# Gated MLPs by fast matrix products: factors of the second token half made form by form between the products, and the down-projection's sums moved to VectorE

## Chip, cores and metric

The kernel runs on one core of a Trainium2 chip. The metric is the device time of one execution in microseconds. The core has TensorE (PE, matmuls into PSUM), VectorE (DVE), ScalarE (ACT), GpSimd (POOL) and the queue of SyncE (SP) that issues its transfers between HBM and SBUF.

## What is computed

A trunk of two layers over 1024 tokens of 1024 channels in float32: a gated linear attention layer, then a differential attention layer on shared keys and values, each followed by the same kind of gated MLP with a causal convolution of width 3 over the tokens. The change touches the two MLPs alone. From the reference:

```python
def conv_ffn(h, w_in, conv_w, conv_b, w_out):
    S = h.shape[1]
    u = h @ w_in                                  # 1024 -> 2 x 2816
    up = jnp.pad(u, ((0, 0), (CONV_WIDTH - 1, 0), (0, 0)))
    c = sum(up[:, j:j + S, :] * conv_w[j] for j in range(CONV_WIDTH)) + conv_b
    a, g = jnp.split(c, 2, axis=-1)
    return (jax.nn.silu(g) * a) @ w_out           # 2816 -> 1024
...
h = h + conv_ffn(rmsnorm(h, ffn_norm_w[l]), ffn_w_in[l], ffn_conv_w[l], ffn_conv_b[l], ffn_w_out[l])
```

## The kernel before

Channels lie on the 128 partitions and tokens on the free axis, in two halves of 512 tokens. A float32 product is made of three matmuls: each operand x is split into a rounded high part (copied by ScalarE) and a low part x - high (made by VectorE), and high x high, low x high and high x low are summed in PSUM. `halves` makes such a pair for a tile of 128 x 512: one ScalarE row, one VectorE row.

Both projections of an MLP use a seven-product scheme for 2 x 2 block matrices (Winograd's form of Strassen's). In the up-projection a block product is formed of sums of weight blocks (the pieces `wp`, made by `pieces` and `pieces_by_form`, their sums on GpSimd) and sums of blocks of the normalised stream (the factors `xp`). The blocks of the stream are channel halves and token halves: b11 and a21 (first token half), b12 and b22 (second). The seven factor forms are called "11", "21", "22", "t1", "t2", "t3", "t4"; each has four tiles. "11" and "21" need the first token half alone and are ready when the MLP starts. The other five need the second half, whose RMS norm is finished by `nm.begin(1)` and `nm.end(1)` during the first two products; `nm.factors1()` then makes all five forms in one go, 8 scalings (`scaled`), 16 subtractions in place and 20 pairs of halves.

A product is 12 matmuls of 128 x 512 (four tiles, three matmuls each). `product(i, n)` takes the next weight piece with `take()`, which also makes the piece four products ahead (`AHEAD = WIN`), and `mid(i, n, o)` adds the result to the tiles `u` of pair i. The first two tile pairs (i = 0, 1) are computed together, in the order of forms 11, 21, 22, t1, t2, t3, t4, each form for both pairs: these are products 0 to 13, and the text counts them so. From product 14 on, pairs i = 2 to 21 follow one by one, with the convolutions (`conv_a`, `conv_g0`, `conv_g1`) of the pair before; beside i = 2 run the convolutions of pairs 0 and 1.

In the down-projection seven products n = 0 to 6 run over 11 steps j each; a step is four units (d) of three matmuls. `factors(n, j)` is called two steps ahead and makes the weight factor `lp` and the activation factor `rp` of a step; E[j] and O[j] are the even and odd tile of W_out (`wo`), and for n = 1, 2, 4 a factor is a sum of them (`ws` or `wo` in place). `gather(n, d)` takes the outputs of product n to the residual tiles `h` (from `ht`): products 0 and 1 are copied to `pt` tiles t1 and t2 by ScalarE, and with product 2 the shared sums p1 (product 0 + 2) and p7 (p1 + product 1) go to the four output blocks h11, h12, h21, h22.

The orders of PE, ACT and the SP queue are those of the program text. DVE and POOL rows are put in order by the framework's scheduler, but run in that order. All work tiles come from one pool of 44 slots, U(...).

## Time and profile before

| | us |
|---|---|
| median of three runs | 2475.18 (2474.60 to 2475.31) |
| the profiled execution | 2473.61 |
| its span, first to last instruction | 2471.9 |
| PE busy | 2341.2 (95%) |
| DVE busy | 1899.2 (77%) |
| ACT busy | 1039.0 (42%) |
| POOL busy | 837.4 (34%) |
| mean granted TensorE clock | 0.978 of 2.4 GHz |

Busy shares are means over stages with different limits; what a stage waits for is read from that stage. The first MLP begins near 455 us and ends near 1130, the second runs from 1763 to the end. A timeline row gives start, duration, engine, line, operation and tiles (out<-in, buffer numbers left out), and in brackets the idle time ahead of it and what ended it. A DVE or ACT row that stands among others of its engine overlaps the next by 0.08 to 0.1 us, so rows are counted from start to start.

### The profile page before, as it was taken

What the parts mean: (1) busy time and instruction counts of PE and PEld (TensorE: products, weight loads), DVE (VectorE), ACT (ScalarE), POOL (GpSimd) and SP (SyncE); (2) the same over time, 40 slices, a digit from 0 to 9 for tenths busy, and PEclk for the clock granted to TensorE, in tenths of its full rate; (3) what the DMA queues carried; (4) which work ended last, traced back from release to release, by engine and by line L of the source; (5) the groups of instructions that cost most, each with busy time, mean ns of one, the idle gap of its engine ahead of it and who ended that gap; (6) DMA issues with size and microseconds to landing.
All of it is one profiled execution on the core that took longest, in us unless ns stands there. A gap on an engine that the chain in (4) does not pass through costs nothing. (4 is left out here: it accounts for less than half of the span.)

```text
span 2471.9 us, 29625 instructions
## 1 busy us (share of the span) xinstructions
PE 2341.2 (95%) x10926; PEld 1888.5 (76%) x10926; DVE 1899.2 (77%) x2509; ACT 1039.0 (42%) x1856; POOL 837.4 (34%) x659
## 2 busy tenths in 40 slices
PE   8999999799999998999999999899789999998998
PEld 6878877577888886788877777787667888886786
DVE  7454454779999998957148888776779999999966
ACT  5433442433444344444124555544334433343453
POOL 3210101145554428400004444522036545436501
PEclk9999999899999999999999999999989999999999
DMA  4011224122333356324243333522113323256422
GB/s 178 1 52 69 70 93 149 42 68 95 111 110 99 111 200 230 117 71 165 81 138 106 107 111 95 182 75 94 67 34 120 119 82 111 92 192 222 144 88 98
DMA packets 101426, 271.22 MB, mean 110 GB/s; under 512 B 10273, under 2 KB 23201, under 8 KB 101281
## 3 DMA queue, kind: packets, MB, share of 16 engines
q1 hardware_dynamic: 101280, 269.34, 32.3%
q8 instruction: 85, 1.39, 0.2%
q14 instruction: 61, 0.49, 0.1%
HBM read 184.89 MB, written 76.02 MB: 106 GB/s over the span
## 5 line engine op out<-in xcount | busy, mean ns | idle before, releaser
L896 PE MATMUL pf<-xp,wp 128*128 128x512 f32 x1232 | 489.2, 397 | 37.4 <-ACT wp L205 33.2
L897 PE MATMUL pf<-xp,wp 128*128 128x512 f32 x1232 | 489.0, 397 | 7.1 <-DVE wp L114 7.1
L898 PE MATMUL pf<-xp,wp 128*128 128x512 f32 x1232 | 488.6, 397 | 0.0
L896 PEld LDWEIGHTS pf<-xp,wp 128*128 128x128 f32 x1232 | 233.1, 189 | 94.0 <-ACT wp L205 34.3
L897 PEld LDWEIGHTS pf<-xp,wp 128*128 128x128 f32 x1232 | 233.1, 189 | 64.3 <-DVE wp L114 9.1
L898 PEld LDWEIGHTS pf<-xp,wp 128*128 128x128 f32 x1232 | 233.0, 189 | 54.8
L1007 PE MATMUL out<-rp,lp 128*128 128x512 f32 (+1 forms) x632 | 251.1, 397 | 19.1 <-DVE rp L114 18.8
L1006 PE MATMUL out<-rp,lp 128*128 128x512 f32 (+1 forms) x632 | 250.1, 396 | 6.3 <-DVE lp L114 6.3
L114 DVE SCALAR_TENSOR_TENSOR c<-u,cv,c 128x1024 f32<-128x1024 f32 x176 | 244.7, 1392 | 7.6 <-ACT c L903 7.6
L1005 PE MATMUL out<-rp,lp 128*128 128x512 f32 (+1 forms) x632 | 249.9, 395 | 0.6 <-ACT rp L205 0.6
L111 DVE TENSOR_TENSOR u<-pf,u 128x512 f32<-128x512 f32 x300 | 200.4, 679 | 28.3 <-PE pf L898 20.1
L114 DVE SCALAR_TENSOR_TENSOR wp<-raw,wp 128x512 fp32r<-128x512 f32 x180 | 203.0, 1139 | 12.9 <-ACT wp L205 12.9
L275 PE MATMUL pf<-xh,wh 128*128 128x512 f32 x458 | 187.5, 409 | 10.7 <-ACT wh L195 9.7
L276 PE MATMUL pf<-xh,wl 128*128 128x512 f32 x458 | 181.9, 397 | 1.2 <-DVE wl L114 1.2
L277 PE MATMUL pf<-xl,wh 128*128 128x512 f32 x458 | 181.4, 396 | 0.0
L1007 PEld LDWEIGHTS out<-rp,lp 128*128 128x128 f32 x632 | 121.3, 192 | 51.6 <-DVE rp L114 24.6
L111 POOL TENSOR_TENSOR rs_y<-rs_m,nhalf 128x4 f32<-128x4 f32 (+2 forms) x26 | 31.9, 1226 | 370.9 <-DVE rs_m L291 301.7
L923 ACT ACTIVATE c<-c 128x1024 f32<-128x1024 f32 x44 | 46.7, 1061 | 255.7 <-DVE c L114 255.7
L114 DVE SCALAR_TENSOR_TENSOR wp<-wt,wp 128x512 fp32r<-128x512 f32 x128 | 153.6, 1204 | 0.0
L1006 PEld LDWEIGHTS out<-rp,lp 128*128 128x128 f32 x632 | 120.8, 191 | 36.8 <-DVE lp L114 9.8
L111 POOL TENSOR_TENSOR wt<-raw,wt 128x512 f32<-128x512 f32 x40 | 57.0, 1425 | 254.5 <-DVE wp L114 254.5
L1005 PEld LDWEIGHTS out<-rp,lp 128*128 128x128 f32 x632 | 121.3, 192 | 27.6 <-ACT rp L205 1.1
(252 smaller groups left out, 5170.5 us busy)
## 6 DMA issues: line engine op xcount, KB each, us to landing
raw<-in_w_in SPq DMA_DIRECT2D x88, 512.0 KB, 4.2
tr<-td SPq DMA_DIRECT2D x70, 512.0 KB, 4.1
td<-c SPq DMA_DIRECT2D x44, 512.0 KB, 2.8
wo<-in_w_out SPq DMA_DIRECT2D x44, 512.0 KB, 8.5
raw<-in_w_gla SPq DMA_DIRECT2D x24, 512.0 KB, 5.9
h<-hs SPq DMA_DIRECT2D x24, 512.0 KB, 6.5
td<-mt SPq DMA_DIRECT2D x22, 512.0 KB, 3.8
hs<-h SPq DMA_DIRECT2D x32, 256.0 KB, 2.0
```

The lines of the kernel that those rows point to most:

```text
L111: eng.tensor_tensor(out=o, in0=a, in1=b, op=op)
L114: eng.scalar_tensor_tensor(out=o, in0=a, scalar=s, in1=b, op0=op0, op1=op1)
L275: PE.matmul(o, wh[:, k], xh[:, H(hf)], start=(k == 0), stop=False)
L276: PE.matmul(o, wl[:, k], xh[:, H(hf)], start=False, stop=False)
L277: PE.matmul(o, wh[:, k], xl[:, H(hf)], start=False, stop=(k == ND - 1))
L896: PE.matmul(o, wh, xh, start=(k == 0), stop=False)
L897: PE.matmul(o, wl, xh, start=False, stop=False)
L898: PE.matmul(o, wh, xl, start=False, stop=(k == ND // 2 - 1))
L923: ACT.activation(gt, gt, AF.Silu)
L1005: PE.matmul(o, wh, xh, start=(j == 0 or cut and j == NJ - LASTF), stop=False)
L1006: PE.matmul(o, wl, xh, start=False, stop=False)
L1007: PE.matmul(o, wh, xl, start=False, stop=(j == NJ - 1 or cut and j == NJ - LASTF - 1))
```

## The change

`factors1` becomes `factor1(q)`, which makes one form. `WHEN` says behind which product each is made: "22" behind product 1, t1 behind 2, t2 behind 4, t3 behind 6, t4 behind 8; the scalings of the second token half are made with "22" (four) and t1 (four). The `mid` of a product now stands behind the factor that is made there.

In the down-projection the sums of `factors` for n = 1, 2 and 4 go from GpSimd to VectorE. Product 2's outputs are copied by ScalarE to tiles t3, as those of products 0 and 1 are, and its twelve sums with the shared terms leave `gather`: `shared(d, part)` makes them on VectorE, one part behind each of the steps j = 1 to 8 of product 3.

```diff
@@ -35,6 +35,7 @@
 EX = 2
 SK = 1
 PF = (4, 4)
+WHEN = {1: "22", 2: "t1", 4: "t2", 6: "t3", 8: "t4"}
 CV = (2, 3, 4, 5)
 VGP = 4
 OGP = 4
@@ -392,27 +393,22 @@
 
             self.f["11" if d < ND // 2 else "21"].append(halves(self.scaled(d, 0), "xp"))
 
-        def factors1(self):
-
-            f, n = self.f, ND // 2
-            a1, a2 = ([self.x[q * n + d][:, H(0)] for d in range(n)] for q in range(2))
-            b2 = [self.scaled(n + d, 1) for d in range(n)]
+        def factor1(self, q):
+
+            n = ND // 2
+            a1, a2 = ([self.x[p * n + d][:, H(0)] for d in range(n)] for p in range(2))
+            b1, b2 = ([self.x[p * n + d][:, H(1)] for d in range(n)] for p in range(2))
+            if q in ("22", "t1"):
+                for d in range(n):
+                    self.scaled(d if q == "t1" else n + d, 1)
+            to, x, y = {"22": (b2, None, None), "t1": (a1, b1, a1), "t2": (a1, b2, a1), "t3": (b1, b2, b1),
+                        "t4": (a2, a2, a1)}[q]
             for d in range(n):
-                f["22"].append(halves(b2[d], "xp"))
-            b1 = [self.scaled(d, 1) for d in range(n)]
-            for d in range(n):
-                tt(DVE, a1[d], b1[d], a1[d], ALU.subtract)
-                f["t1"].append(halves(a1[d], "xp"))
-            for d in range(n):
-                tt(DVE, a1[d], b2[d], a1[d], ALU.subtract)
-                f["t2"].append(halves(a1[d], "xp"))
-            for d in range(n):
-                tt(DVE, b1[d], b2[d], b1[d], ALU.subtract)
-                f["t3"].append(halves(b1[d], "xp"))
-            for d in range(n):
-                tt(DVE, a2[d], a2[d], a1[d], ALU.subtract)
-                f["t4"].append(halves(a2[d], "xp"))
-            self.x.clear()
+                if x is not None:
+                    tt(DVE, to[d], x[d], y[d], ALU.subtract)
+                self.f[q].append(halves(to[d], "xp"))
+            if q == "t4":
+                self.x.clear()
 
     class Late:
 
@@ -954,7 +950,7 @@
         CG = (2, 4, 6, 7, 10)
         SRC = (0, 1, 5, 4, 3, 6, 2)
         E, O, lp, rp, rraw, acc, ht = {}, {}, {}, {}, {}, {}, []
-        t1, t2 = {}, {}
+        t1, t2, t3 = {}, {}, {}
 
         def load_w(f):
             t = (O if f % 2 else E)[f // 2] = U("wo")
@@ -974,16 +970,16 @@
                 x = a[0]
             elif n == 1:
                 x = U("ws")[:, H(0)]
-                tt(POOL, x, a[0], a[1], ALU.subtract)
+                tt(DVE, x, a[0], a[1], ALU.subtract)
             elif n == 2:
                 x = a[0]
-                tt(POOL, a[1], a[1], b[1], ALU.add)
+                tt(DVE, a[1], a[1], b[1], ALU.add)
                 tt(DVE, x, a[1], x, ALU.subtract)
             elif n == 3:
                 x = a[1]
             elif n == 4:
                 x = a[0]
-                tt(POOL, x, b[0], x, ALU.subtract)
+                tt(DVE, x, b[0], x, ALU.subtract)
                 del E[j]
             elif n == 5:
                 x = b[1]
@@ -1006,27 +1002,32 @@
             PE.matmul(o, wl, xh, start=False, stop=False)
             PE.matmul(o, wh, xl, start=False, stop=(j == NJ - 1 or cut and j == NJ - LASTF - 1))
 
+        def shared(d, part):
+
+            h11, h12, h21, h22 = (ht[k][:, H(q)] for k in (d, d + 4) for q in range(2))
+            p1, p7, p6 = (t[d // 2][:, H(d % 2)] for t in (t1, t2, t3))
+            if part == 0:
+                tt(DVE, p6, p1, p6, ALU.add)
+                tt(DVE, p7, p6, p7, ALU.add)
+                tt(DVE, h12, h12, p6, ALU.add)
+                return
+            tt(DVE, h22, h22, p7, ALU.add)
+            tt(DVE, h21, h21, p7, ALU.add)
+            tt(DVE, h11, h11, p1, ALU.add)
+            if d % 2 == 1:
+                del t1[d // 2], t2[d // 2], t3[d // 2]
+
         def gather(n, d, sl=H(0)):
 
             o = acc.pop((n, d))
-            if n < 2:
-                t = (t1, t2)[n]
+            if n < 3:
+                t = (t1, t2, t3)[n]
                 if d % 2 == 0:
                     t[d // 2] = U("pt")
                 ACT.activation(t[d // 2][:, H(d % 2)], o, AF.Copy)
                 return
             h11, h12, h21, h22 = (ht[k][:, H(q)] for k in (d, d + 4) for q in range(2))
-            if n == 2:
-                p1, p7 = t1[d // 2][:, H(d % 2)], t2[d // 2][:, H(d % 2)]
-                tt(POOL, h11, h11, p1, ALU.add)
-                tt(DVE, p1, o, p1, ALU.add)
-                tt(DVE, p7, p1, p7, ALU.add)
-                tt(POOL, h12, h12, p1, ALU.add)
-                tt(POOL, h21, h21, p7, ALU.add)
-                tt(DVE, h22, h22, p7, ALU.add)
-                if d % 2 == 1:
-                    del t1[d // 2], t2[d // 2]
-            elif n == 3:
+            if n == 3:
                 tt(DVE, h12, o, h12, ALU.add)
                 tt(DVE, h22, o, h22, ALU.add)
             elif n == 4:
@@ -1039,12 +1040,14 @@
 
         AHEAD = WIN
         for k, (n, i) in enumerate((n, i) for n in (0, 2, 6, 4, 1, 3, 5) for i in range(2)):
-            mid(i, n, product(i, n))
+            o = product(i, n)
             if k == 0:
                 nm.begin(1)
             if k == 1:
                 nm.end(1)
-                nm.factors1()
+            if k in WHEN:
+                nm.factor1(WHEN[k])
+            mid(i, n, o)
         for i in range(2, NF):
             for p, n in enumerate(range(7)):
                 if i == NF - 1:
@@ -1110,6 +1113,8 @@
             for d in range(4):
                 unit(n, j, d)
             del lp[n, j], rp[n, j]
+            if n == 3 and 1 <= j < 9:
+                shared((j - 1) % 4, (j - 1) // 4)
             if j == NJ - 1:
                 for d in range(4):
                     gather(n, d)
```

The order of ScalarE at the start of an MLP's up-projection, before: the last five of the 20 factor copies (`xp`), then the weight pieces (`wp`) of products 6 to 9 with the copies of products 4 and 5 (`u`) between them.

```order
L205 ACTIVATE xp_3589<-h_2961 128x512
L205 ACTIVATE xp_3593<-h_2987 128x512
L205 ACTIVATE xp_3597<-h_3038 128x512
L205 ACTIVATE xp_3601<-h_3125 128x512
L205 ACTIVATE wp_3604<-wt_3084 128x512
L205 ACTIVATE wp_3625<-wt_3088 128x512
L205 ACTIVATE wp_3642<-wt_3084 128x512
L854 ACTIVATE u_3457<-pf_3645 128x512
L205 ACTIVATE wp_3659<-wt_3088 128x512
```

The same place after the change, from the first copy for form "22" on.

```order
L206 ACTIVATE xp_3523<-h_2961 128x512
L206 ACTIVATE xp_3526<-h_2987 128x512
L206 ACTIVATE xp_3529<-h_3038 128x512
L206 ACTIVATE xp_3532<-h_3125 128x512
L846 ACTIVATE u_3490<-pf_3496 128x512
L206 ACTIVATE wp_3536<-wt_3084 128x512
L206 ACTIVATE xp_3561<-h_2950 128x512
L206 ACTIVATE xp_3565<-h_2974 128x512
L206 ACTIVATE xp_3569<-h_3000 128x512
L206 ACTIVATE xp_3573<-h_3082 128x512
L206 ACTIVATE wp_3577<-wt_3088 128x512
L206 ACTIVATE wp_3594<-wt_3084 128x512
```

Product 6's piece (the first `wp<-wt`) stands behind four factor copies, and the pieces of products 7 and 8 behind four more.

GpSimd at the start of product 1 of the first MLP's down-projection, before: the sum `ws` of each step and the first sum of product 2, in turn.

```order
L111 TENSOR_TENSOR ws_7006<-wo_6671 128x512
L111 TENSOR_TENSOR wo_6671<-wo_6671,wo_6982 128x512
L111 TENSOR_TENSOR ws_7032<-wo_6690 128x512
L111 TENSOR_TENSOR wo_6690<-wo_6690,wo_7002 128x512
L111 TENSOR_TENSOR ws_7062<-wo_6713 128x512
L111 TENSOR_TENSOR wo_6713<-wo_6713,wo_7030 128x512
```

VectorE at the same place, before, from the last row of product 0 (`rp<-c`) on.

```order
L114 SCALAR_TENSOR_TENSOR rp_6987<-c_6709,rp_6987 128x512
L114 SCALAR_TENSOR_TENSOR lp_7008<-ws_7006,lp_7008 128x512
L114 SCALAR_TENSOR_TENSOR rp_7011<-tr_6962,rp_7011 128x512
L111 TENSOR_TENSOR wo_6671<-wo_6671 128x512
L111 TENSOR_TENSOR wo_6690<-wo_6690 128x512
L114 SCALAR_TENSOR_TENSOR lp_7034<-ws_7032,lp_7034 128x512
L114 SCALAR_TENSOR_TENSOR rp_7037<-tr_6962,rp_7037 128x512
L111 TENSOR_TENSOR wo_6713<-wo_6713 128x512
```

VectorE there after the change; the rows of GpSimd are gone.

```order
L115 SCALAR_TENSOR_TENSOR rp_6987<-c_6709,rp_6987 128x512
L112 TENSOR_TENSOR ws_7006<-wo_6671 128x512
L112 TENSOR_TENSOR wo_6671<-wo_6671,wo_6982 128x512
L115 SCALAR_TENSOR_TENSOR lp_7008<-ws_7006,lp_7008 128x512
L115 SCALAR_TENSOR_TENSOR rp_7011<-tr_6962,rp_7011 128x512
L112 TENSOR_TENSOR wo_6671<-wo_6671 128x512
L112 TENSOR_TENSOR ws_7032<-wo_6690 128x512
L112 TENSOR_TENSOR wo_6690<-wo_6690,wo_7002 128x512
L115 SCALAR_TENSOR_TENSOR lp_7034<-ws_7032,lp_7034 128x512
L115 SCALAR_TENSOR_TENSOR rp_7037<-tr_6962,rp_7037 128x512
L112 TENSOR_TENSOR wo_6690<-wo_6690 128x512
```

A step of product 1 on VectorE is now five rows: `ws`, the add with the odd tile, `lp`, `rp`, and product 2's subtraction.

VectorE at the start of product 3, before: the shared output sums of product 2 (tiles `pt` and `h`) between `lp` and `rp` of step 3.

```order
L114 SCALAR_TENSOR_TENSOR lp_7612<-wo_6735,lp_7612 128x512
L111 TENSOR_TENSOR pt_7052<-out_7334,pt_7052 128x512
L111 TENSOR_TENSOR pt_7052<-out_7338,pt_7052 128x512
L111 TENSOR_TENSOR pt_7316<-pt_7052,pt_7316 128x512 x2
L111 TENSOR_TENSOR h_7350<-h_7350,pt_7316 128x512
L111 TENSOR_TENSOR h_7372<-h_7372,pt_7316 128x512
L111 TENSOR_TENSOR pt_7055<-out_7342,pt_7055 128x512
L111 TENSOR_TENSOR pt_7055<-out_7346,pt_7055 128x512
L111 TENSOR_TENSOR pt_7319<-pt_7055,pt_7319 128x512 x2
L111 TENSOR_TENSOR h_7396<-h_7396,pt_7319 128x512
L111 TENSOR_TENSOR h_7418<-h_7418,pt_7319 128x512
L114 SCALAR_TENSOR_TENSOR rp_7615<-tr_7526,rp_7615 128x512
```

After the change, from `lp` of step 1 of product 3 on.

```order
L115 SCALAR_TENSOR_TENSOR lp_7546<-wo_6690,lp_7546 128x512
L115 SCALAR_TENSOR_TENSOR rp_7549<-tr_7484,rp_7549 128x512
L112 TENSOR_TENSOR pt_7564<-pt_7052,pt_7564 128x512 x2
L112 TENSOR_TENSOR pt_7316<-pt_7564,pt_7316 128x512
L112 TENSOR_TENSOR h_7248<-h_7248,pt_7564 128x512
L112 TENSOR_TENSOR pt_7316<-pt_7564,pt_7316 128x512
L115 SCALAR_TENSOR_TENSOR lp_7572<-wo_6713,lp_7572 128x512
L115 SCALAR_TENSOR_TENSOR rp_7575<-tr_7526,rp_7575 128x512
L115 SCALAR_TENSOR_TENSOR lp_7594<-wo_6735,lp_7594 128x512
L115 SCALAR_TENSOR_TENSOR rp_7597<-tr_7526,rp_7597 128x512
L115 SCALAR_TENSOR_TENSOR lp_7617<-wo_6752,lp_7617 128x512
L115 SCALAR_TENSOR_TENSOR rp_7620<-tr_7570,rp_7620 128x512
```

The block is split: five rows stand ahead of step 2's `lp` and `rp`, the others come between later steps.

## Rows read from the trace of the kernel before

**Rows 1.** Waits of PE over the span: us in total, times, longest.

```profile
PE pf L896 <- ACT wp L205: 33.2, 2, 16.6
PE out L1007 <- DVE rp L114: 18.8, 10, 5.6
...
PE pf L897 <- DVE wp L114: 7.1, 4, 2.0
PE out L1006 <- DVE lp L114: 6.3, 8, 1.3
```

**Rows 2.** Timeline of PE, start of the second MLP's up-projection.

```profile
1800.36 0.79 PE L896 MATMUL pf<-xp,wp 128*128 128x512 f32 x1 [16.62 <-ACT wp L205]
1802.75 0.80 PE L897 MATMUL pf<-xp,wp 128*128 128x512 f32 x1 [1.60 <-DVE wp L114]
1803.34 0.63 PE L898 MATMUL pf<-xp,wp 128*128 128x512 f32 x1
...
1808.03 0.39 PE L897 MATMUL pf<-xp,wp 128*128 128x512 f32 x1
1808.26 0.40 PE L898 MATMUL pf<-xp,wp 128*128 128x512 f32 x1
...
1874.30 0.51 PE L897 MATMUL pf<-xp,wp 128*128 128x512 f32 x1 [1.88 <-DVE wp L114]
```

**Rows 3.** Timeline of ACT, same stretch: product 6's piece, product 14's copy.

```profile
1799.70 1.65 ACT L205 ACTIVATE wp<-wt 128x512 fp32r<-128x512 f32 x3
...
1830.31 0.60 ACT L868 ACTIVATE u<-pf 128x512 f32<-128x512 f32 x1 [13.34 <-PE pf L898]
```

**Rows 4.** Timeline of DVE, same stretch: first and last factor rows, then pieces.

```profile
1772.64 2.73 DVE L114 SCALAR_TENSOR_TENSOR h<-h,gains_sb,rb 128x512 f32<-128x512 f32 x4 [1.12 <-PE rb L308]
1775.28 2.49 DVE L114 SCALAR_TENSOR_TENSOR xp<-h,xp 128x512 fp32r<-128x512 f32 x4
...
1798.98 1.28 DVE L111 TENSOR_TENSOR u<-pf,u 128x512 f32<-128x512 f32 x2
...
1800.95 4.64 DVE L114 SCALAR_TENSOR_TENSOR wp<-wt,wp 128x512 fp32r<-128x512 f32 x4
```

**Rows 5.** Windows, down-projections: length, busy by engine, PE clock, DMA share, GB/s.

```profile
950.00:1000.00 50.00, 42.85 (x168) 32.50 (x169) 45.63 (x41) 19.69 (x37) 39.09 (x24) 0.97 0.53 187
1000.00:1050.00 50.00, 44.40 (x180) 35.39 (x179) 47.07 (x56) 23.52 (x41) 19.74 (x13) 0.93 0.37 107
...
2250.00:2300.00 50.00, 43.59 (x165) 32.60 (x164) 45.59 (x39) 21.07 (x39) 40.65 (x26) 0.93 0.63 229
2300.00:2350.00 50.00, 44.43 (x181) 35.45 (x180) 47.64 (x52) 19.99 (x36) 25.29 (x16) 0.93 0.35 104
```

**Rows 6.** Timelines of DVE, ACT and POOL, second MLP, end of product 0, product 1.

```profile
2240.72 1.78 DVE L114 SCALAR_TENSOR_TENSOR rp<-c,rp 128x512 fp32r<-128x512 f32 x1
...
2250.17 1.22 ACT L1016 ACTIVATE pt<-out 128x512 f32<-128x512 f32 x2 [0.15 <-PE out L1007]
...
2250.19 1.63 POOL L111 TENSOR_TENSOR wo<-wo,wo 128x512 f32<-128x512 f32 x1
...
2254.00 1.78 DVE L111 TENSOR_TENSOR wo<-wo 128x512 f32<-128x512 f32 x1
2255.70 1.78 DVE L114 SCALAR_TENSOR_TENSOR lp<-ws,lp 128x512 fp32r<-128x512 f32 x1
```

**Rows 7.** Timelines of DVE and PE, second MLP, product 3.

```profile
2322.68 1.28 DVE L111 TENSOR_TENSOR pt<-out,pt 128x512 f32<-128x512 f32 x2
...
2337.86 0.68 DVE L114 SCALAR_TENSOR_TENSOR rp<-tr,rp 128x512 fp32r<-128x512 f32 x1
...
2338.59 0.80 PE L1007 MATMUL out<-rp,lp 128*128 128x512 f32 x1 [5.57 <-DVE rp L114]
```

**Rows 8.** Timeline of POOL, start of the second MLP's up-projection.

```profile
1799.20 1.28 POOL L111 TENSOR_TENSOR wt<-raw 128x512 f32<-128x512 f32 x1 [29.08 <-DVE h L111]
1800.56 1.59 POOL L111 TENSOR_TENSOR wt<-wt,raw 128x512 f32<-128x512 f32 x1
```

## The prediction

> **What bounds the kernel now.** I read the waits of TensorE first, over the whole span: who made it stand still, and for how long [rows 1]. Four of these lines belong to the two MLPs: 33.2 us in two waits for a piece of up-projection weights, 7.1 us for the low half of such a piece, and 18.8 + 6.3 us for the factors rp and lp of the down-projection. That is 65 of the 2471.9 us. The rest of the MLPs runs TensorE without a gap, so these 65 us, and the half clock that follows them, are all that an edit of this kind can win.
>
> Then I went to the two places. At the up-projection's start the second MLP's timeline [rows 2] shows TensorE, with six products done, idle for 16.62 us up to 1800.36, a second wait of 1.60, and then 0.427 us from matmul to matmul until 1808.03 ((1808.03 - 1803.34) / 11): half clock, 1.2 GHz, against 0.23 at the full 2.4 just after. So 16.6 + 1.6 idle and 12 x (0.427 - 0.23) = 2.4 lost to the clock, 20.5 us; the first MLP has the same two waits (the counts of 2 and 4 in [rows 1]). What was late is product 6's weight piece, which ScalarE copied at 1799.70, right after the last of its 20 copies for factors [rows 3]. Those copies waited for VectorE, which from 1772.64 to 1798.98 made nothing but factors [rows 4].
>
> In the down-projection I read windows of 50 us [rows 5]. In each MLP the two windows around products 1 and 3 hold PE busy of 42.6 to 44.4 of 50: 12.8 us idle in the first MLP, 12.0 in the second, and a mean clock of 0.93 to 0.97, which is another (0.03 + 0.07) x 50 = 5.0 and 7.0 us at most (some of that low clock falls in the idle time itself; from the half-rate bursts that follow the waits I count 4 and 6). So 17 to 18 us for each MLP, say 17.5. Why: in product 1 each VectorE row takes 1.70 us from start to start [rows 6], although a low half of the same size takes 0.60 when GpSimd rests (four in 2.49, the last of them 0.68 long [rows 4]); GpSimd is in a sum all that time. Three such rows for a step are 5.1 us, and a step of TensorE is 12 matmuls, 2.78 us. At product 3 the twelve output sums of product 2 stand in one block on VectorE, 2322.68 to 2337.86, and TensorE waits 5.57 us for the rp row behind it [rows 7].
>
> **The change, part by part.** *Factors.* No instruction is added: 8 scalings, 16 subtractions and 20 low halves for each MLP, as before. What moves is the place of the weight pieces. The order of ScalarE after the change has product 6's piece behind four factor copies instead of twenty, product 7's behind eight, and so on; on VectorE products' sums and pieces stand between the forms. I work the new start out on the second MLP's clock, VectorE from 1772.64 in the changed order: 0.66 for a scaling (four in 2.73), 0.60 for every other row [rows 4]. The last low half of t1 is the 23rd row: 8 x 0.66 + 15 x 0.60 = 14.3, 1786.9. Twelve rows on ends t2 (1794.1), ten more t3 (1800.1), eleven more t4 (1806.7). TensorE is free for product 6 at 1783.7 and needs t1's last low half eleven matmuls on, at 1786.2: it waits 0.7 and ends product 6 at 1787.2, 7 at 1790.0. Product 8 ends 0.2 behind t2, 1794.4; product 10 behind t3, 1800.4; 11 (its piece at 1801.4) at 1804.0; 12 at 1807.0; 13 behind its piece (1807.4) at 1810.0; 14 at 1812.8. Before, product 14 ended at 1830.3, as ScalarE's copy of it shows [rows 3]. That is 17.5 us earlier, with VectorE now the one that paces products 6 to 13.
>
> Two things take from it. GpSimd's sums for the next weights begin when the last h row is done (1799.20 before [rows 8]) and will now fall on a VectorE with no idle time. The price: four low halves beside two such sums took 4.64 us where 2.41 is their time [rows 4, 8], 1.1 us for each GpSimd row. Four of them (three sums and a first output sum) can stand before t4's last half and product 13's piece: 4.4 us. None is the lower bound, all eight of that stretch, 8.8, the upper. The Trainium skill (page SBUF — State Buffer, section Who interferes with whom) says that a VectorE instruction with two SBUF inputs and a GpSimd instruction that reads SBUF lock each other out for a whole instruction; by that rule four rows of 1.3 to 1.7 us would cost 5.2 to 6.8 and my sum would be 1 to 2 us less for each MLP. The rows give 1.1, and I use that. Second, the convolutions of two tile pairs at once: even with VectorE idle before them, TensorE waits 1.88 us at 1874.30 [rows 2] as they drain. VectorE arrives with some backlog now, so I add 1 us (0 to 2). Gain at the start: 17.5 - 4.4 - 1 = 12 us for each MLP, between 6.5 and 17.5.
>
> *Down-projection.* Out of GpSimd go 33 sums of weights and 12 of outputs for each MLP; VectorE gets them. ScalarE gets four copies (product 2's outputs, 0.6 each, in a queue that waits for TensorE there anyway). In product 1 a step on VectorE becomes ws, the add, lp, rp, the subtraction: five rows at 0.60, 3.0 us; with GpSimd quiet nothing stretches them. That is more than TensorE's 2.78, so the start matters: VectorE ends product 0's last row at 2242.4 and TensorE product 0 at 2250.9 (the second pair of copies of its outputs starts at 2250.17, one unit of 0.7 before the end) [rows 6]. Step 0 is ready after four rows, at 2244.8, 6 us early; each step gives back 0.2, or 0.3 with the wait for ScalarE's copy between ws and lp, so step 10 is still some 2.5 to 4 us early. Should its tiles come free only two steps ahead, that lead is 3 and is used up at the end: 0.5 us. Behind each add is queued the next lp and rp, and the add needs the odd weight tile from memory: GpSimd's third add began at 2250.19 without a wait [rows 6], and VectorE will come to that add at 2249.6, so I charge nothing for it (0.6 at most). Product 3: of the block one part of five rows (3.0 us) stays ahead of step 2's lp and rp, which start about 0.7 us after product 2's end and so are ready near 4.9 us, for a need at 5.6: hidden, with 0.7 to spare; if the copies come one unit later this wait is 1 us. The other rows go between later steps, at most four a step: 6 x 0.60 = 3.6 us, above 2.78 for two or three steps, covered by the two steps of lead. I take 1 us of the 17.5 as left: 16.5 for each MLP, between 12 and 17.5.
>
> *Sum.* 2 x (12 + 16.5) = 57 us. The profiled execution took 2473.61 (span 2471.9 and 1.7 around it); the median of the runs is 2475.18, 1.6 above. 2473.6 - 57 = 2416.6, and with the 1.6, **2418.2 us**.
>
> **Rivals.** *The start gives it back.* VectorE has hardly a free microsecond in the up-projection after the start, so a backlog that it brings into the convolutions would come out as waits like the one at 1874.30. If all of the contention and 4 us more of such waits stand, the start yields 17.5 - 8.8 - 4 = 5 us: 2475.2 - 2 x (5 + 16.5) = 2432. For it: that wait exists already, with VectorE idle ahead. Against: the free time of VectorE before the convolutions shrinks, but ScalarE's first convolution row still waits for product 14's copy [rows 3], which gives VectorE 2 us to catch up.
>
> *The clock swings.* TensorE now stops for about 1 us at every second product. In product 1 of the down-projection, waits of that size left a mean clock of 0.93 [rows 5]. If all of products 6 to 13 ran at the half rate, they would take 8 x 12 x 0.427 = 41 us, not the 22.3 of the full rate; the lead of 17.5 would be 0, and the time 2475.2 - 33 = 2442. Against: half rate came in bursts, and while VectorE paces, a burst is partly hidden. The Trainium skill (TensorE: Matmul & The Clock Gate, section HAM oscillation — how this bites in real kernels) tells of kernels in which repeated waits between groups of matmuls held the clock down, which is this rival; here the windows agree that it can happen [rows 5].
>
> *Slower.* VectorE runs in order, and the adds of product 1 now put it behind loads. If each add waited for its odd tile, lp and rp of all later steps would wait too, and through them the release of the next loaded tile. It decides where it eats 28.5 us for each MLP, (28.5 + 6) / 11 = 3.1 us for each step beyond the lead of 6. At 4 us a step the time would be 2418 + 2 x (44 - 6) = 2494. Against it: the add that comes soonest after its load found it there [rows 6].
>
> *Nothing to tell.* Both gains lost together to other waits, 2471 to 2480: no row speaks for it.
>
> **How the numbers follow.** Forecast, both stalls gone but for the parts named, 2404 to 2428: 0.70. The start gives back, 2428 to 2438: 0.14. Clock, 2438 to 2447: 0.07. Better than 2404: 0.03. Within 5 us (0.2%, what a measurement of this kernel can tell): 0.02. Slower: 0.04. The ends: 2 x (17.5 + 17.5) = 70 gives 2405, 2 x (6.5 + 12) = 37 gives 2438; I write 2403 to 2440, which leaves some 0.15 outside.
>
> **What would show it.** Right: no wait of over 3 us for a weight piece at the start of either MLP, many of 0.3 to 1.5 for factors and pieces in products 6 to 13; VectorE rows of 0.6 to 0.7 us all through product 1 of the down-projection and GpSimd idle in it; no 5.6 us wait in product 3. Wrong: a new row of some us in which TensorE waits for a wp in the first convolutions (the first rival), a granted clock near 0.5 over the start (the second), VectorE waiting for wo loads (the third).

## The result and the profile after

The changed kernel takes 2415.8 us (median of four runs, 2411.1 to 2420.9) against 2474.9 us before: 59.1 us less, a ratio of 0.976, with a 95% interval of 0.975 to 0.977. The forecast was 2418.2, in a range of 2403 to 2440. The profiled execution of the changed kernel is one of the longer ones, 2419.2 us with a span of 2417.1.

In the changed kernel the three matmuls of an up-projection product are L892 to L894 (before L896 to L898), those of the down-projection L1001 to L1003 (L1005 to L1007), VectorE's sums L112 and low halves L115 (L111, L114), and ScalarE's copies L206 (L205). The waits of TensorE over the whole span, to be set beside [rows 1] (us in total, times, longest):

```profile
PE pf L893 <- DVE wp L115: 12.7, 10, 1.9
...
PE pf L894 <- DVE xp L115: 1.5, 4, 0.4
PE out L1001 <- ACT rp L206: 1.4, 1, 1.4
...
PE pf L892 <- ACT xp L206: 1.2, 2, 0.6
```

The two waits of 16.6 us for a piece are gone, and so are all 18 waits of the down-projections for `rp` and `lp` of VectorE. Most of what is left of the MLPs' waits is ten of at most 1.9 us for the low half of a piece, five in each MLP; six small ones for factors of the up-projection come to 2.7 us in all. The windows of the down-projections, as in [rows 5], but over the places where the changed kernel has them (products 1 and 3 run from 929 to 960 and from 991 to 1021 in the first MLP, from 2214 to 2245 and from 2276 to 2307 in the second):

```profile
900.00:950.00 50.00, 50.00 (x217) 40.37 (x216) 47.63 (x66) 22.27 (x37) 6.63 (x4) 1.00 0.79 297
950.00:1000.00 50.00, 50.00 (x216) 40.29 (x215) 42.32 (x70) 27.55 (x50) 0.00 (x0) 1.00 0.48 157
1000.00:1050.00 50.00, 50.00 (x218) 40.60 (x217) 34.23 (x58) 19.75 (x35) 0.00 (x0) 1.00 0.35 107
...
2200.00:2250.00 50.00, 50.00 (x217) 40.44 (x216) 47.88 (x73) 25.05 (x45) 5.01 (x3) 1.00 0.79 288
2250.00:2300.00 50.00, 50.00 (x216) 40.35 (x215) 42.76 (x72) 25.51 (x47) 0.00 (x0) 1.00 0.40 122
```

PE is busy for 50 of 50 us at a granted clock of 1.00, where it had 42.9 to 44.4 at 0.93 to 0.97, and GpSimd (the fifth engine column) is silent in them from product 1 on: its last rows begin at 918.67 and 2204.05, in product 0. The start of the second MLP's up-projection on TensorE; these are all of its waits of 0.25 us and more:

```profile
1736.96 0.47 PE L892 MATMUL pf<-xp,wp 128*128 128x512 f32 x1 [4.17 <-DVE h L112]
...
1760.59 0.51 PE L894 MATMUL pf<-xp,wp 128*128 128x512 f32 x1 [0.34 <-DVE xp L115]
...
1766.73 0.50 PE L892 MATMUL pf<-xp,wp 128*128 128x512 f32 x1 [0.64 <-ACT xp L206]
...
1767.82 0.50 PE L894 MATMUL pf<-xp,wp 128*128 128x512 f32 x1 [0.35 <-DVE xp L115]
...
1775.57 0.50 PE L893 MATMUL pf<-xp,wp 128*128 128x512 f32 x1 [0.95 <-DVE wp L115]
...
1806.37 0.50 PE L893 MATMUL pf<-xp,wp 128*128 128x512 f32 x1 [1.62 <-DVE wp L115]
...
1813.25 0.50 PE L893 MATMUL pf<-xp,wp 128*128 128x512 f32 x1 [1.00 <-DVE wp L115]
...
1817.40 0.50 PE L893 MATMUL pf<-xp,wp 128*128 128x512 f32 x1 [0.85 <-DVE wp L115]
...
1836.32 0.52 PE L893 MATMUL pf<-xp,wp 128*128 128x512 f32 x1 [1.88 <-DVE wp L115]
```

Products 6 to 13 now have four small waits, 2.3 us in all. Then come three new ones at 1806 to 1817, in the first convolutions; the wait of 1.88 us behind them was there before [rows 2].

To see where time came from and went I followed TensorE's **lead**: for each product (12 matmuls) the time from the first matmul of its projection to the product's last matmul, in the kernel before minus in the changed one. It does not depend on where the projection stands in the span. For product 14 two rows show it, the first matmul before,

```profile
1763.47 0.61 PE L896 MATMUL pf<-xp,wp 128*128 128x512 f32 x1 [4.16 <-DVE h L111]
```

and the copy of product 14 after:

```profile
1787.21 0.60 ACT L864 ACTIVATE u<-pf 128x512 f32<-128x512 f32 x1 [0.35 <-PE pf L894]
```

Before, that copy came at 1830.31 [rows 3], so the lead is (1830.31 - 1763.47) - (1787.21 - 1736.96) = 66.8 - 50.3 = 16.6 us. Worked out in the same way from the matmuls' timelines (the two lines of each half are the two MLPs of the profiled execution):

```
up-projection, after product   7     9    11    14    19    21    23    25    41   153 (last)
  first MLP                  20.3  18.6  17.1  16.6  16.6  14.1  12.8  11.6  11.6  12.1
  second MLP                 20.2  18.5  17.0  16.6  16.7  14.2  12.8  11.5  10.0   9.6
down-projection, in product   0 (end)   1 (middle)   1 (end)   2 (end)   3 (middle)  last
  first MLP                      0         6.5         12.0      11.9      20.3      20.1
  second MLP                     0         6.5         12.0      12.1      20.3      19.4
```

Two things stand out. The down-projection gives 20.3 us, all at products 1 and 3; of the 0.9 us that the second MLP loses behind them, 0.8 is its wait for ScalarE's copy of `rp`, 1.40 us where it was 0.62. The start gives 16.6 us, of which 5.1 are handed back between products 20 and 25. The loss of 1.5 us in the second MLP behind product 25 is a burst of nine matmuls at half clock after the wait at 1836.32, 0.425 us from start to start.

The parts of the span (from the first matmul of an up-projection to the last of its down-projection for an MLP):

```
us                 ahead   first MLP   between   second MLP   behind    span
before             457.6     691.2      614.6      696.0       12.5    2471.9
changed            455.7     659.0      622.3      666.9       13.2    2417.1
difference           1.9      32.2       -7.7       29.1       -0.7      54.8
```

The MLPs are 61.3 us shorter. The attention between them, whose code is the same, is 7.7 us longer in this execution. The first experiment asks about that.

### The profile page after: what moved, and what is told of

Same layout as the page of the kernel before. It is cut to its first block, busy times and chain, and to the rows that moved or that the text cites. A ratio compares the mean times of both kernels' runs of the same rounds, so it can differ in the third digit from the quotient of the medians.

```text
span 2417.1 us, 29569 instructions
## 1 busy us (share of the span) xinstructions
PE 2333.6 (97%) x10926; PEld 1882.5 (78%) x10926; DVE 1866.0 (77%) x2599; ACT 1040.6 (43%) x1864; POOL 692.5 (29%) x569
## 5 line engine op out<-in xcount | busy, mean ns | idle before, releaser
L892 PE MATMUL pf<-xp,wp 128*128 128x512 f32 x1232 | 488.2, 396 | 5.7 <-DVE h L112 4.2
L894 PE MATMUL pf<-xp,wp 128*128 128x512 f32 x1232 | 487.9, 396 | 1.8 <-DVE xp L115 1.5
L892 PEld LDWEIGHTS pf<-xp,wp 128*128 128x128 f32 x1232 | 232.1, 188 | 63.6 <-issue 4.6
L894 PEld LDWEIGHTS pf<-xp,wp 128*128 128x128 f32 x1232 | 232.1, 188 | 59.0 <-DVE xp L115 5.6
L1001 PE MATMUL out<-rp,lp 128*128 128x512 f32 (+1 forms) x632 | 246.3, 390 | 1.4 <-ACT rp L206 1.4
L115 DVE SCALAR_TENSOR_TENSOR c<-u,cv,c 128x1024 f32<-128x1024 f32 x176 | 246.4, 1402 | 0.0
L1003 PE MATMUL out<-rp,lp 128*128 128x512 f32 (+1 forms) x632 | 246.0, 389 | 0.0
L1002 PE MATMUL out<-rp,lp 128*128 128x512 f32 (+1 forms) x632 | 245.6, 389 | 0.0
L115 DVE SCALAR_TENSOR_TENSOR wp<-raw,wp 128x512 fp32r<-128x512 f32 x180 | 202.0, 1131 | 14.0 <-ACT wp L206 13.8
L112 DVE TENSOR_TENSOR u<-pf,u 128x512 f32<-128x512 f32 x300 | 200.5, 680 | 15.4 <-PE pf L894 10.4
L112 POOL TENSOR_TENSOR rs_y<-rs_m,nhalf 128x4 f32<-128x4 f32 (+2 forms) x26 | 31.9, 1225 | 524.2 <-DVE rs_m L292 457.1
L115 DVE SCALAR_TENSOR_TENSOR wp<-wt,wp 128x512 fp32r<-128x512 f32 x128 | 150.4, 1176 | 2.5 <-ACT wp L206 2.5
L1001 PEld LDWEIGHTS out<-rp,lp 128*128 128x128 f32 x632 | 118.7, 188 | 28.3 <-ACT rp L206 1.8
L1003 PEld LDWEIGHTS out<-rp,lp 128*128 128x128 f32 x632 | 118.7, 188 | 27.5 <-DVE rp L115 0.8
L1002 PEld LDWEIGHTS out<-rp,lp 128*128 128x128 f32 x632 | 118.8, 188 | 26.7
L112 POOL TENSOR_TENSOR wt<-raw,wt 128x512 f32<-128x512 f32 x40 | 57.0, 1424 | 253.8 <-DVE wp L115 253.8
```

Of the source, the lines that this page charges most:

```text
L112: eng.tensor_tensor(out=o, in0=a, in1=b, op=op)
L115: eng.scalar_tensor_tensor(out=o, in0=a, scalar=s, in1=b, op0=op0, op1=op1)
L892: PE.matmul(o, wh, xh, start=(k == 0), stop=False)
L894: PE.matmul(o, wh, xl, start=False, stop=(k == ND // 2 - 1))
L1001: PE.matmul(o, wh, xh, start=(j == 0 or cut and j == NJ - LASTF), stop=False)
L1002: PE.matmul(o, wl, xh, start=False, stop=False)
```

## The experiments

**The changed kernel again.** No edit. It is the control for the runs below.

> The changed kernel once more, as the control of this group: it tells what lies in the part that no line of the change touches. In the profiled execution the two MLPs came out 60.5 us shorter (32.2 and 28.3 with the last rows), but the attention part between them 7.7 us longer (622.3 for 614.6), 7.0 of it as lost clock. Theory A (bursts of half clock fall differently from execution to execution): the four times of the changed kernel lay in two groups, 2411 to 2412 and 2419 to 2421; this profile will show either an attention part near 622 with a time near 2420, or one near 614 with a time near 2412; the MLPs as before within 1 us. Theory B (the changed MLP leaves something late that attention pays for): the attention part is near 622 again at every time, and a time of 2412 has its gain elsewhere.

Measured: 2415.8 us (2414.5 to 2419.5), ratio 0.976 (0.974 to 0.977); profiled at 2414.5. Its MLPs are 659.0 and 664.8 us, without the half-clock burst in the second. The attention part is 619.4: between the two values that the theories named.

**The kernel before, twice more**, for the same question.

> The kernel before once more, one look, for the attention part between the MLPs, which no line of the change touches. Six profiles of the changed kernel and of its variants have 618.2 to 622.3 us there, the only profile of before 614.6. Theory A (half-clock bursts fall by chance): this one lies somewhere in 614 to 622, as the time of before has lain between 2470.8 and 2479.9. Theory B (with the change the attention part is always some 4 us longer): 614 to 615 again.

> The same kernel as in the run ahead of it and the same question: under theory A the attention part of this execution differs from that of the last by some us, under B both have 614 to 615.

Measured: 2470.9 and 2478.4 us, with 614.5 and 618.3 us between the MLPs; the MLPs themselves repeat within 0.9 us. So before, too, the part between scatters. Where it is long, it is mostly the clock: over windows of 10 us, the sum of (1 - granted clock) x 10 is 11.9 us where the part takes 614.6, 17.2 where it takes 618.3 (both before), 17.0 at 619.4 and 18.9 at 622.3 (both changed), while TensorE's idle time there is 33.3 to 34.9 us in all four. So the scatter of theory A exists. Theory B is not excluded: over all nine profiles of the changed kernel and the variants the part takes 617.3 to 622.3, 619.1 in the mean, and the mean of the three of before is 615.8. Of these 3.3 us, 2.1 are lost clock by the same count and 1.0 is idle time of TensorE.

**The down-projection's part alone.** The start is as before (`factors1` in one go, the copy ahead of the factors).

```
-            o = product(i, n)
+            mid(i, n, product(i, n))
...
-            if k in WHEN:
-                nm.factor1(WHEN[k])
-            mid(i, n, o)
+                nm.factors1()
```

> The down-projection's part of the change alone; the factors of the second token half are made in one go, as before. Theory (the two parts do not touch each other): the lead in the down-projection is the 20.2 us of the changed kernel in each MLP (12.0 by the end of product 1, 8.2 at product 3), the up-projection's start waits 16.6 us as before; time 2475 - 40 = 2435, from 2432 to 2443 with the clock's scatter in attention. Rival (part of the 20 us belongs to the start, for instance because VectorE comes into the down-projection earlier): a lead clearly under 20, time above 2445.

Measured: 2439.2 us (2432.3 to 2442.4) against 2476.1 in the same group (kernels timed together), ratio 0.984 (0.982 to 0.987). The lead in the down-projection is 12.1 us at the end of product 1 and 20.5 in the middle of product 3, in both MLPs, as in the changed kernel; the two 16.6 us waits stand where they stood. The down-projection's gain does not need the new start.

**The weight sums alone.** The kernel before, with these three sums moved, and nothing else.

```
-                tt(POOL, x, a[0], a[1], ALU.subtract)
+                tt(DVE, x, a[0], a[1], ALU.subtract)
...
-                tt(POOL, a[1], a[1], b[1], ALU.add)
+                tt(DVE, a[1], a[1], b[1], ALU.add)
...
-                tt(POOL, x, b[0], x, ALU.subtract)
+                tt(DVE, x, b[0], x, ALU.subtract)
```

> The kernel before, with only the weight sums of the down-projection (ws, wo) on VectorE instead of GpSimd; factors, output copies and the block of shared output sums as before. Theory (the two stalls are separate: GpSimd's sums make product 1, the block makes product 3): lead 12.0 by the end of product 1, nothing more at product 3, where TensorE waits 5 to 6 us as before; 12 us for each MLP, time about 2451. Rival 1 (the block was long because GpSimd's sums stretched it too): part of the 8.2 us at product 3 comes as well, lead 14 to 18, time 2440 to 2448. Rival 2 (five rows a step and the 12 rows at once): product 3 waits longer than before, lead under 11.

Measured: 2452.1 us (2450.1 to 2454.4) against 2476.8, ratio 0.991 (0.989 to 0.992). The lead is 12.1 at the end of product 1 and 12.6 in the middle of product 3. Its waits of TensorE:

```profile
PE pf L896 <- ACT wp L205: 33.3, 2, 16.6
...
PE out L1007 <- DVE rp L114: 11.2, 2, 5.6
...
PE pf L897 <- DVE wp L114: 7.1, 4, 2.0
```

The two 5.6 us waits at product 3 are untouched, and those of product 1 are gone, although VectorE has more rows there than before. So the 20.3 us are 12.1 for the weight sums that left GpSimd and some 8 for the rest of the edit, the block of output sums. Rival 2 falls, and rival 1 for the weight sums: the block, on VectorE from 2298.26 to 2313.42 in this run, is as long without them, 15.2 us. But it is GpSimd that makes it so long, with its own twelve output sums; VectorE's rows of the first half of the block, and GpSimd's beside them:

```profile
2298.26 1.28 DVE L111 TENSOR_TENSOR pt<-out,pt 128x512 f32<-128x512 f32 x2
2299.46 3.10 DVE L111 TENSOR_TENSOR pt<-pt,pt 128x512 f32<-128x512 f32 x2
2302.48 3.48 DVE L111 TENSOR_TENSOR h<-h,pt 128x512 f32<-128x512 f32 x2
```

```profile
2299.02 6.39 POOL L111 TENSOR_TENSOR h<-h,pt 128x512 f32<-128x512 f32 x4 [23.54 <-DVE pt L111]
```

At 0.60 a row the twelve rows would take 7.2 us, 8.0 less. In the change all 24 sums are VectorE's, which in one block would be 14.4 us, nearly the old length (an estimate, from 0.60 a row). So taking them off GpSimd would hardly have been enough without the spreading; whether spreading alone, with GpSimd's part left, would have been, no run shows.

**What gives 5.1 us back at the start.** In the changed kernel VectorE, ahead of its first convolution row (`c<-u,cv,c`):

```profile
1782.06 1.19 DVE L115 SCALAR_TENSOR_TENSOR wp<-raw,wp 128x512 fp32r<-128x512 f32 x1
1783.17 0.68 DVE L112 TENSOR_TENSOR u<-pf,u 128x512 f32<-128x512 f32 x1
1785.11 1.11 DVE L115 SCALAR_TENSOR_TENSOR wp<-wt,wp 128x512 fp32r<-128x512 f32 x1 [1.26 <-ACT wp L206]
1787.41 0.69 DVE L112 TENSOR_TENSOR u<-pf,u 128x512 f32<-128x512 f32 x1 [1.20 <-POOL u L112]
1788.02 1.17 DVE L115 SCALAR_TENSOR_TENSOR wp<-raw,wp 128x512 fp32r<-128x512 f32 x1
...
1792.09 0.69 DVE L112 TENSOR_TENSOR u<-pf,u 128x512 f32<-128x512 f32 x1 [1.20 <-POOL u L112]
1792.70 1.16 DVE L115 SCALAR_TENSOR_TENSOR wp<-wt,wp 128x512 fp32r<-128x512 f32 x1
1793.78 2.31 DVE L115 SCALAR_TENSOR_TENSOR c<-u,cv,c 128x1024 f32<-128x1024 f32 x1
```

GpSimd in the same stretch:

```profile
1779.81 2.89 POOL L112 TENSOR_TENSOR u<-u,u 128x512 f32<-128x512 f32 x1 [4.84 <-DVE u L112]
1782.66 1.75 POOL L112 TENSOR_TENSOR wt<-wt,raw 128x512 f32<-128x512 f32 x1
1784.36 1.31 POOL L112 TENSOR_TENSOR raw<-raw,raw 128x512 f32<-128x512 f32 x1
...
1785.68 1.70 POOL L112 TENSOR_TENSOR u<-u,u 128x512 f32<-128x512 f32 x1
1787.34 1.29 POOL L112 TENSOR_TENSOR u<-u 128x512 f32<-128x512 f32 x1
1788.60 1.74 POOL L112 TENSOR_TENSOR wt<-raw,wt 128x512 f32<-128x512 f32 x1
1790.30 1.76 POOL L112 TENSOR_TENSOR u<-u 128x512 f32<-128x512 f32 x1
```

VectorE waits 3.7 us for GpSimd (1.26 + 1.20 + 1.20; ScalarE's `wp` waits for GpSimd's `wt`), and its `wp` rows take 1.1 to 1.2 us instead of 0.68. Its first convolution row comes 56.8 us after the projection's first matmul (1793.78 - 1736.96), before it was 68.6: a gain of 11.8, where TensorE's lead at product 14 is 16.6. How much of the loss comes from GpSimd (its queue, or its mere presence beside VectorE), and how much is VectorE's own work?

*The sums of `u` on VectorE* (in `mid`, for the first two tile pairs):

```
-                    tt(POOL, a2, a2, g1, ALU.add)
+                    tt(DVE, a2, a2, g1, ALU.add)
...
-                    tt(POOL, g2, g2, g1, ALU.add)
+                    tt(DVE, g2, g2, g1, ALU.add)
```

> The changed kernel, with the four sums of the first two tile pairs (u<-u,u) of each MLP on VectorE, which GpSimd makes at the start. In the changed kernel TensorE leads by 16.6 us at product 14 and gives back 5.1 in the first convolutions. Theory A (GpSimd's queue): the sums stand on GpSimd behind weight sums that wait there, VectorE waits twice 1.2 us for them and 1.3 us for a piece, so the first convolution starts 4.8 us late against product 14. Without them in that queue the waits go, four rows of 0.6 us come: first convolution 1.5 to 4 us earlier, the lead after the convolutions 13 to 15 instead of 11.5, time 3 to 7 us less. Theory B (VectorE's own work in the two convolutions at once is more than TensorE's seven products, whoever makes the sums): the lead after the convolutions stays at 11.5 or falls by the 2.4 us of the four rows; time the same to 5 us more.

Measured: 2411.4 us (2408.6 to 2413.0) where the changed kernel had 2415.8 in the same group; ratios to before 0.974 (0.972 to 0.975) and 0.976. The lead after the convolutions is 12.8 instead of 11.5: 1.3 us, less than theory A asked for and more than B. VectorE waits for GpSimd no more, but at product 14 the lead is only 14.4. Of the 4.4 us of the medians the MLPs have only 0.9 in the two profiles (2.4 without a half-clock burst that this one has and the control has not).

*The first convolutions spread over nine products:*

```
-                    (conv_a, conv_g0, conv_g1, conv_a, conv_g0, conv_g1, lambda i: spill_m())[p](p // 3)
+                    if p in (0, 1, 3, 4, 6):
+                        (conv_a, conv_g0, None, conv_g1, conv_a, None, conv_g0)[p](p // 4)
                     continue
+                if i == 3 and p == 0:
+                    conv_g1(1)
+                if i == 3 and p == 1:
+                    spill_m()
```

> The changed kernel, with the convolutions of the first two tile pairs spread over nine products instead of six (the second pair's gate and its sums for the mix come in the group behind). Theory A (the first convolution starts late, behind GpSimd): the first wait for a piece, 1.6 us, stays nearly as it is, since the start of the first convolution does not move; later waits (1.0, 0.85, 1.9) fall by a part; lead after the convolutions 12 to 14. Theory B (two convolutions at once are too much for VectorE): all four waits shrink together, lead 14 to 16.5, time 5 to 10 us less than the changed kernel.

Measured: 2416.6 us (2415.9 to 2417.9), no gain. The lead is still 15.0 at product 25, falls to 9.2 by product 29 and stands at 10.5 from product 33 on. Both theories missed. Three rows of this run, of VectorE, GpSimd and TensorE, show what stands at the place:

```profile
1824.52 4.54 DVE L115 SCALAR_TENSOR_TENSOR c<-u,cv,c 128x1024 f32<-128x1024 f32 x2
...
1824.12 1.63 POOL L112 TENSOR_TENSOR wt<-wt,raw 128x512 f32<-128x512 f32 x1
...
1829.71 0.50 PE L893 MATMUL pf<-xp,wp 128*128 128x512 f32 x1 [2.02 <-DVE wp L115]
```

Two convolution rows take 4.54 us, 2.27 each instead of 1.27, beside three GpSimd sums in a row. The waits only moved to where GpSimd works next. Behind the last of these rows stand eight matmuls at half clock, 0.43 us from start to start, in both MLPs; without this burst of 1.5 us the lead would be 12.0, at the edge of theory A (an estimate).

*Eight low halves off VectorE* (those of t2 and t3; ScalarE writes a second copy there):

```
+                if q in ("t2", "t3"):
+                    t = U("xp", F32R)
+                    ACT.activation(t[:, H(0)], to[d], AF.Copy)
+                    ACT.activation(t[:, H(1)], to[d], AF.Copy, scale=1.0 / 4096)
+                    self.f[q].append(t)
+                    continue
                 self.f[q].append(halves(to[d], "xp"))
```

> The changed kernel, in which ScalarE writes a scaled copy in place of the low half of the eight factors of t2 and t3 (leaves out: the remainder that VectorE computes there; the products of these two forms are not exact). VectorE loses 8 rows of 0.60 = 4.8 us in products 6 to 11 of each MLP, ScalarE gets 8 copies of 0.5. Theory B (VectorE's rows between the second half's norm and the first convolution set when that convolution starts, and with it what TensorE gives back): the lead after the convolutions rises from 11.6 by 3.5 to 5, to 15 to 16.5, the waits in products 8 to 13 go; time 7 to 10 us below the changed kernel. Theory A (GpSimd's queue): the first convolution still waits for the sums of u behind the weight sums, lead 11.6 to 13, time 0 to 3 us less.

Measured: 2407.4 us (2405.6 to 2408.9), ratio 0.972 (0.971 to 0.974); lead after the convolutions 13.4. Of the 4.8 us taken off VectorE 1.9 arrive: short of B, above A. (The median is 8.4 us below the control's; of that the MLPs have 3.7 in the two profiles, and 2.1 lie in the attention part.) The rest went into one row, the low halves of t4; below it the GpSimd rows beside it:

```profile
1769.08 6.87 DVE L115 SCALAR_TENSOR_TENSOR xp<-h,xp 128x512 fp32r<-128x512 f32 x4
```

```profile
1770.28 1.74 POOL L112 TENSOR_TENSOR wt<-raw 128x512 f32<-128x512 f32 x1
1772.09 1.61 POOL L112 TENSOR_TENSOR wt<-wt,raw 128x512 f32<-128x512 f32 x1
1773.66 1.74 POOL L112 TENSOR_TENSOR raw<-raw,raw 128x512 f32<-128x512 f32 x1
```

Four rows that take 2.49 us alone [rows 4] took 6.87: 1.7 us each, which is GpSimd's own pace. VectorE, earlier by the rows it had lost, met GpSimd's sums there and lost 4.4 us. That made theory C.

*GpSimd silent in the start:* left out are the sums of `u` above and the weight sums of the next two pairs.

```
-        a11, a12, s3, a22, s1, s2 = sums(ra, rg)
+        quiet[0] -= 1
+        if quiet[0] >= 0:
+            a11, a12, s3, a22 = (t[:, H(q)] for t in (ra, rg) for q in range(2))
+            s1, s2 = a22, a12
+        else:
+            a11, a12, s3, a22, s1, s2 = sums(ra, rg)
...
-        tt(POOL, s2, a12, s2, ALU.subtract)
+        if quiet[0] < 0:
+            tt(POOL, s2, a12, s2, ALU.subtract)
...
-                    tt(POOL, a2, a2, g1, ALU.add)
...
-                    tt(POOL, g2, g2, g1, ALU.add)
```

> The changed kernel with GpSimd silent at each up-projection's start: left out are the four sums of u of the first two tile pairs and the eight weight sums of the next two pairs (their pieces are made from the plain weights), so VectorE has the same rows as in the changed kernel and GpSimd twelve fewer. In the changed kernel VectorE comes to the first convolution 4.8 us late against product 14, and TensorE's lead falls from 16.6 to 11.5. Theory C (GpSimd beside VectorE: rows with two SBUF inputs take 1.1 to 1.7 instead of 0.6 us, and VectorE waits 3.7 us for GpSimd's results): lead after the convolutions 15.5 to 17, no wp row above 0.7 us in the start, time 8 to 11 us below the changed kernel. Theory B (the convolutions of two pairs at once are VectorE's own work, GpSimd or not): lead 11.5 to 13, time 0 to 3 us less.

Measured: 2398.0 us (2397.4 to 2402.1), ratio 0.970 (0.968 to 0.971), 17.8 us below the control's median. The lead is 17.1 at product 14 and still 17.1 at product 25, in both MLPs; at the end of the projection 17.9 and 18.4. The MLPs take 652.8 and 657.7 us, 13.3 less than in the control run of the changed kernel (by the ratios to before it is 0.0060, 15 us). VectorE's `wp` rows of the start, grouped (count: shortest, median, longest in ns), and behind them, from the timeline, its first convolution row:

```profile
L115 DVE SCALAR_TENSOR_TENSOR wp<-raw,wp x10: 681/685/689, 1762.7 to 1783.5; 128x512 fp32r<-128x512 f32 x10
```

```profile
1782.33 1.28 DVE L115 SCALAR_TENSOR_TENSOR c<-u,cv,c 128x1024 f32<-128x1024 f32 x1 [1.53 <-ACT c L904]
```

Every row is at 0.68 to 0.69, and VectorE even waits 1.53 us for ScalarE before it convolves. With the same rows on VectorE, and the same two convolutions at once, nothing is given back. Theory B falls; GpSimd is the whole of the 5.1 us, and 0.5 more ahead of product 14. How the 5.1 us divide between VectorE's waits for GpSimd's results and the rows that GpSimd stretches is not shown, since this run takes both away.

*The next pair's weight sums on VectorE too* (to the edit of `u` above is added, for one pair):

```
-        tt(POOL, s1, a21, a22, ALU.add)
+        tt(eng, s1, a21, a22, ALU.add)
...
+        first[0] -= 1
+        eng = DVE if first[0] >= 0 else POOL
```

> The variant with the four sums of u on VectorE, and beside it the four weight sums of the first pair behind the start (product 16 on) on VectorE too; exact. Against that variant VectorE gets 4 x 0.60 = 2.4 us more, and the rows that GpSimd's three sums stretched there (+0.5, +0.5, +1.1, +0.5 = 2.6) go back to 0.6. Theory C (contention is worth as much as the rows themselves): lead after the convolutions 12.5 to 13.5, like the 12.8 of that variant, time 2409 to 2413. Theory B (VectorE's own row time alone counts): lead 10.5, time 4 us more than that variant.

Measured: 2410.8 us (2408.8 to 2411.5), ratio 0.975 (0.973 to 0.976); lead after the convolutions 13.0, as C has it. Four more rows on VectorE cost nothing, since the rows beside them are quick again. Its MLPs (657.0 and 664.4) are 2.4 us shorter in all than the control's, and the ratios to before differ by 0.0011, 2.7 us; the intervals of the two ratios overlap, so by the time alone it is not shown to be better than the changed kernel.

In all these runs but the spread one, TensorE's lead after the convolutions is what VectorE's first convolution row gained (both in us, second MLP; the row's time less that of the projection's first matmul, against the 68.6 of before):

```
                      first convolution row after first matmul   gained   TensorE's lead after product 25
changed                                56.8                       11.8        11.5
u sums on VectorE                      56.1                       12.5        12.7
u and weight sums                      55.9                       12.7        12.9
eight low halves off                   54.9                       13.7        13.4
GpSimd silent                          51.6                       17.0        17.1
```

## Why the prediction was right

**The sum** was 57 us and came to 59.1 by the medians. Its steps hold, with one term too small: the MLPs, of which alone it speaks, gave 61.3 us in the first profile and 63.4 in the control's. That the time came out only 2.4 us from the forecast is in part luck, since the attention part, which the sum leaves out, took some 3 us back.

**The products of the start** came as worked out from VectorE's row counts. The forecast had the ends of products 6, 7, 8, 10, 11, 12, 13 and 14 at 1787.2, 1790.0, 1794.4, 1800.4, 1804.0, 1807.0, 1810.0 and 1812.8 of the second MLP's clock before; measured, shifted to that clock, they are 1787.3, 1790.3, 1794.6, 1800.6, 1804.7, 1807.9, 1810.7 and 1813.5. The lead of 17.5 was 16.6, or 17.1 with GpSimd silent.

**What is taken back** was 4.4 for GpSimd's rows and 1 for the convolutions, 5.4 in all. It is 5.6 us (17.1 - 11.5), and all of it is GpSimd's. That the two figures agree is luck, since I counted four rows at 1.1 us and 1 us for the convolutions, where the runs have twelve rows at about half a us and nothing for the convolutions. The place, too, was wrong: I let GpSimd hold up TensorE ahead of product 14, and there it cost 0.5. It held up VectorE, which had 3.7 us of waits for GpSimd and longer rows before its first convolution, and TensorE paid in products 20 to 24. The 1.1 us for each GpSimd row is right where the rows stand close: in the eight-low-halves run four VectorE rows lost 4.4. Over the twelve rows of the start it is 5.6 / 12 = 0.47. The 12 us for each start came out as 12.1 and 9.6 in the first profile, 12.1 and 11.3 in the control's.

The sentence on the Trainium skill (SBUF — State Buffer, section Who interferes with whom) can be set beside rows. The page has VectorE and GpSimd lock each other out for whole instructions if VectorE reads two operands from SBUF and GpSimd reads SBUF too, and not if VectorE has at most one operand there. The rows agree on which of them suffer: `xp<-h,xp` stands at GpSimd's pace, 1.7 us, while `u<-pf,u`, whose `pf` lies in PSUM, takes 0.68 and 0.69 between GpSimd's rows. What I made of the rule, 5.2 to 6.8 us for four rows, was too much, since a row that goes at GpSimd's pace costs that pace less the 0.6 us it takes anyway: 4 x 1.1, and 4.4 were measured.

**The down-projection** was put at 16.5 for each MLP and gives 20.3. Here a term was mis-sized: the stall of 17.5 that I read from windows. Counted as start-to-start time above 0.2316 us for a matmul, products 1 and 3 of before lose 20.6 us in the first MLP and 20.5 in the second. The clock was read right: matmuls at half rate lose 4.1 and 5.6 us of it, put at 4 and 6. What was missed is that a wait costs more than its idle time. At 1800.36 [rows 2] it is 16.62 idle, but 16.79 from start to start beyond a matmul's own time. Over the eleven and ten waits of products 1 and 3 this is 2.2 and 2.0 us, and the matmul behind a wait loses another 0.1 us, 0.6 and 0.5 in all. In the first MLP the window also began behind 0.7 us of idle time (13.4, not 12.8). The 1 us that I left standing is 0. Two figures of that working are slightly off, without effect on the sum: the least busy window has 42.85 us [rows 5], not 42.6, and 16.6 + 1.6 + 2.4 is 20.6, not 20.5. The mechanism held row by row. VectorE in the first MLP, first and last step of product 1 and two steps between:

```profile
922.36 0.69 DVE L115 SCALAR_TENSOR_TENSOR lp<-ws,lp 128x512 fp32r<-128x512 f32 x1
922.97 0.68 DVE L115 SCALAR_TENSOR_TENSOR rp<-tr,rp 128x512 fp32r<-128x512 f32 x1
...
943.23 0.68 DVE L112 TENSOR_TENSOR ws<-wo 128x512 f32<-128x512 f32 x1
...
946.25 0.68 DVE L112 TENSOR_TENSOR ws<-wo 128x512 f32<-128x512 f32 x1
...
954.68 0.68 DVE L115 SCALAR_TENSOR_TENSOR rp<-tr,rp 128x512 fp32r<-128x512 f32 x1
```

A step takes 3.02 us (946.25 - 943.23), as forecast. The first step's factors are there at 923.65 for a matmul at 929.11, 5.5 us early (forecast 6); the last step's at 955.36 for 956.98, 1.6 us early (forecast 2.5 to 4). Of the 3.9 us used up, 1.6 are one wait for ScalarE's copy at 930.45; the rest is the 0.24 us by which a step is longer than TensorE's 2.78. By these rows (an estimate) some six more steps would have used up the lead, and one more row in each step a good deal fewer.

**The rivals.** *The start gives it back* had the right mechanism, waits in the first convolutions, but its 13 us were 5. *The clock swings*: from 1750 to 1800 us the granted clock is 1.00, from 1800 to 1850 it is 0.97, with the one burst of 1.5 us. Four of the seven profiles with the new start show such a burst behind a wait in the first convolutions, and so do three of the five with the old. *Slower*: no row of product 1 waits for a loaded tile; VectorE's one wait there, 1.62 us at 930.45, is for ScalarE's copy of `lp`. *Nothing to tell* falls with the result.

**What stays open** is the part between the MLPs, which I had not thought of: about 3 us longer in the mean with the change, some two thirds of it lost clock and one third idle time. No run tells whether this is chance or because attention is entered in another rhythm.

## What to carry to other kernels

An engine that helps another can cost it as much as it does for it. At the start twelve sums on GpSimd cost 5.6 us of TensorE's lead, by way of VectorE, and VectorE would need 12 x 0.6 = 7.2 to make them. In product 1 GpSimd's sums stretched three VectorE rows a step from 1.8 to 5.1 us, while five rows with GpSimd quiet take 3.0. Ahead of product 3 twelve GpSimd sums stretched VectorE's block by 8.0 us. Where both read SBUF, a GpSimd row cost here from 0.5 us, where they met now and then, to 1.1, where they stood close.

When a stall is removed, look for the next place where the same two engines meet, and measure there: a lead that is shown product by product tells at once where it is given back, which one number for the whole kernel does not.

## What the runs showed of the hardware

The time of code that is not touched varies. The attention part took 614.5 to 622.3 us over twelve profiles, with 11.9 us of lost clock in the shortest and 18.9 in the longest, while the two MLPs of the kernel before each repeated within 0.9 us. A change of 5 us in 2400 can't be told from the time of one execution.

A VectorE row that reads two tiles of 128 x 512 from SBUF took 0.60 us from start to start alone and 1.70 beside GpSimd sums that stood back to back; a row with one operand in PSUM stayed 0.68 to 0.69 us long beside them, as it is alone.
